# A second load of x, by positions, for the row sums of squares at the start of a hybrid decoder layer

## The chip, the cores and the metric

One core of one Trainium2 chip runs the whole layer as one program. The metric is device time in microseconds (us), median over runs. The engines are named as in the profile: PE (TensorE matmuls) and PEld (its weight loads), DVE (VectorE), ACT (ScalarE), POOL (GpSimd), SP (SyncE, whose queue issues nearly all DMAs here).

## What is computed

The reference is a layer with two token mixers and a gated MLP, float32, sequence 1024, width 1024. For the change only the first projection and the QK norm matter:

```python
def rmsnorm(x, gain):
    y = x * lax.rsqrt(jnp.mean(x * x, axis=-1, keepdims=True) + NORM_EPS)
    return y * gain

h = rmsnorm(x, mix_norm)
proj = h @ w_in                     # q, k, v, u, s, gate_a, gate_b
q = rmsnorm(q.reshape(B, S, N_Q_HEADS, HEAD_DIM), q_gain)
k = rmsnorm(k.reshape(B, S, N_KV_HEADS, HEAD_DIM), k_gain)
```

After that come banded attention (8 query heads, 2 key heads of 64), a chunked spatial gate, the output projections and a convolutional MLP.

## The kernel before, in words

All products run on PE as three float32r products, high by high, high by low, low by high (`mm3`, lines 91 to 95). So each operand is split: ACT writes the high part (`copy_hi`, line 89), DVE or POOL subtracts it for the low part. x comes transposed, in eight tiles of 128 channels by 1281 columns (a gain, 256 columns of the weights of k and v, 1024 positions).

The norm of x is applied late: the projections of the raw x times the gain are made at once, and the reciprocal root of each position (`rstd`) is multiplied in when results leave PSUM. The stage that the change touches is the first 60 us:

- **x loop** (lines 227 to 256). For each tile k: split the k/v weights (lines 229, 230) and x (233, 234), 24 matmuls into `pkv` (239), squares on ACT, a running sum on DVE (`xsquare`, 211 to 219). SP loads five tiles ahead (`X_AHEAD`). Seven matmuls on a constant stand in front (`warm`, 225).
- **q weights** `wq` in two halves (`rsplit`, 188 to 193): ACT copies, POOL subtracts. The first u weight `u0h`, `u0l` is split on ACT and DVE (258, 259).
- **Sums over channels**: eight small float32 matmuls with a column of ones (`ssq`, 321), then `rstd` (`rsqrt_cols`, 128 to 131: DVE scales, POOL takes the power -0.5).
- **k**: squares of `pkv` on ACT (334), sums on DVE (335), scaled by `rstd` squared (338), a power on POOL for each half, times `rstd` again (346); then `kr` (348), its transposition on PE (`k_trans`, 355), and the splits `k_hi`, `k_lo`, `k_twice` into `kT`.
- **q**, block by block: `q_proj` (24 matmuls into `pq`), `q_sq`, `q_ms`, `q_norm`, `q_trans`, `q_split`. `eps_x` carries the epsilon, scaled to raw x.
- **rms_rows** (135 to 143): `rstd` spread along rows by float32 matmuls into `rb`, copied to `rstd_b` by ACT.
- **v**: `v_evac` (379) and `v_split`. Then scores `sc` (`s_mm`, 439, 442), masks `c` (`s_mask`), and the u projection `pu` (`u_chunk`) as filler.

Each engine works in its own order and waits for semaphores. PE's order is the order of the source everywhere. From line 317 on (`manual_schedule`) the other engines' is too; ahead of it a scheduler orders them. PSUM has four small tiles (pool `psB`: `pq`, `pk`, `pqt`, `rb`, `warm`) and two large ones (`psA`: `pkv`, `sc`, `pu`). A DMA waits at SP until the eighth one ahead of it has landed.

Of the kernel before, what the change touches and what calls it, by code (L numbers as in the profile page):

```python
# [41 lines left out]
def body(ctx, tc, nc, a):  # L42
# [178 lines left out]
    for k in range(X_AHEAD):
        xload(k)
    warm = PH("warm")
    for _ in range(7):
        nc.tensor.matmul(warm[:, 0:128], rstd_b[:, 0:128], rstd_b[:, 0:128], start=True, stop=True)
    xcuts = {0: (slice(0, 256), slice(256, 512), slice(512, 1024))}
    for k in range(8):
        x1 = xr[k]
# [12 lines left out]
        if k > 0:  # L241
            xsquare(k - 1)
        if k + X_AHEAD < 8:
            xload(k + X_AHEAD)
        if k == 2:
            rwq = rload(a["wq"][0], "wq")
            nc.sync.dma_start(ident, a["ident"])
            nc.sync.dma_start(cp, a["cp"])
        if k == 4:
            u_raw = [wload(a["wu"][0], "wu")]  # L250
            nc.sync.dma_start(sink_b, a["sink"])
            nc.sync.dma_start(ali, a["ali"])
        if k == 5:
            rsplit(wq[0], rwq[0], 0)
    xsquare(7)
    rsplit(wq[0], rwq[1], 1)
    u_next = [wst.tile([128, 8, 128], R, tag="wh", name="u0h"), wst.tile([128, 8, 128], R, tag="wl", name="u0l")]
    copy_hi(u_next[0], u_raw[0])
    nc.vector.tensor_tensor(u_next[1], u_raw[0], u_next[0].bitcast(F), op=ALU.subtract)
# [65 lines left out]
    ss8 = pa.tile([128, 8], F, name="ss8")
    nc.vector.tensor_scalar(nsink, sink_b, -1.0, None, op0=ALU.mult)
    nc.vector.tensor_scalar(kgq, cp[:, 184:185], cp[:, 185:186], 0.125, op0=ALU.mult, op1=ALU.mult)
    nc.vector.tensor_copy(ss8, p_ssq[:, 0:16].rearrange("p (s two) -> p s two", two=2)[:, :, 0])
# [1717 lines left out]
```

## Time and profile before

| what | value |
|---|---|
| time, median of 3 runs | 1183.58 us (1183.52 to 1184.87) |
| profiled execution | span 1183.5 us (no other time of it is listed) |
| PE busy | 1170.3 us, 99% of the span |
| PEld, DVE, ACT, POOL busy | 84%, 74%, 48%, 53% |
| mean granted clock of PE | 0.998 |
| chain that ended last | PE 82%, DVE 4%, POOL 3%, ACT 2% |
| HBM read | 146.97 MB |

A group of instructions shows its start, busy time, engine, line, and out<-in; "x24" joins 24 instructions; brackets give the idle time ahead of it on its engine and what ended it. PE's busy time counts a matmul until its modelled end, so starts, not lengths, give its pace.

### The profile page before, as it was taken

What the parts mean: (1) busy time and instruction counts of PE and PEld (TensorE: products, weight loads), DVE (VectorE), ACT (ScalarE), POOL (GpSimd) and SP (SyncE); (2) the same over time, 40 slices, a digit from 0 to 9 for tenths busy, and PEclk for the clock granted to TensorE, in tenths of its full rate; (3) what the DMA queues carried; (4) which work ended last, traced back from release to release, by engine and by line L of the source; (5) the groups of instructions that cost most, each with busy time, mean ns of one, the idle gap of its engine ahead of it and who ended that gap; (6) DMA issues with size and microseconds to landing.
All of it is one profiled execution on the core that took longest, in us unless ns stands there. A gap on an engine that the chain in (4) does not pass through costs nothing.

```text
span 1183.5 us, 15928 instructions
## 1 busy us (share of the span) xinstructions
PE 1170.3 (99%) x5842; PEld 990.4 (84%) x5842; DVE 874.5 (74%) x1037; ACT 566.5 (48%) x878; POOL 631.8 (53%) x435
## 2 busy tenths in 40 slices
PE   8999999999999999999999999999999999999998
PEld 8989989988888878888878888888888888888887
DVE  7798975743536776678788788877888797875674
ACT  8555667644336653335444443444444445425331
POOL 2467685488884764444867677776767541000000
PEclk9999999999999999999999999999999999999999
DMA  7110136157556654454545445455555268975471
GB/s 272 37 55 19 54 130 228 56 168 239 161 160 204 233 193 154 146 176 132 138 129 169 118 149 152 142 141 134 166 137 160 72 219 287 365 232 196 155 231 67
DMA packets 80942, 188.66 MB, mean 159 GB/s; under 512 B 9184, under 2 KB 16864, under 8 KB 80736
## 3 DMA queue, kind: packets, MB, share of 16 engines
q1 hardware_dynamic: 73008, 167.58, 40.7%
q0 software_dynamic: 7456, 15.73, 8.0%
q10 hardware_dynamic: 400, 4.33, 1.1%
q8 instruction: 46, 0.75, 0.3%
q14 instruction: 32, 0.26, 0.1%
HBM read 146.97 MB, written 49.02 MB: 166 GB/s over the span
## 4 chain that ended last, share of the span: by engine, by line
PE 82%; DVE 4%; POOL 3%; ACT 2%; issue 2%; DMA 1%; DVEq 0%; POOLq 0%; SPq 0%; ACTq 0%
PE pz L1060 50%; PE pd L1855 10%; PE pdy L1855 8%; PE px L95 2%; PE px L93 2%; PE px L94 2%; PE pu L95 1%; PE pu L93 1%; PE pu L94 1%; PE pv L517 1%; PE pq L93 1%; PE pq L95 1%; PE pq L94 1%; DVE xa L621 1%; DMA lq<-wup 0%
## 5 line engine op out<-in xcount | busy, mean ns | idle before, releaser
L1060 PE MATMUL pz<-T,qh 128*128 128x512 f32 x472 | 145.6, 390 | 0.0
L1060 PE MATMUL pz<-B,ph 128*128 128x512 f32 x352 | 109.7, 393 | 0.7 <-ACT x L1695 0.7
L1060 PEld LDWEIGHTS pz<-T,qh 128*128 128x128 f32 x472 | 88.4, 188 | 18.6 <-ACT u L885 0.3
L1019 POOL TENSOR_TENSOR pl<-lp,ph 128x1024 fp32r<-128x1024 f32 x30 | 73.2, 2439 | 52.9 <-ACT ph L89 52.9
L1060 PE MATMUL pz<-T,ql 128*128 128x512 f32 x236 | 91.8, 389 | 0.0
L1019 POOL TENSOR_TENSOR ql<-lq,qh 128x1024 fp32r<-128x1024 f32 x30 | 76.8, 2559 | 9.1 <-ACT qh L89 9.1
L1060 PEld LDWEIGHTS pz<-B,ph 128*128 128x128 f32 x352 | 65.1, 188 | 16.7 <-ACT x L1695 3.8
L1078 DVE TENSOR_TENSOR pz<-pz,rstd_b 128x1024 f32<-128x1024 f32 x60 | 73.9, 1232 | 4.6 <-ACT rstd_b L143 2.5
L1060 PE MATMUL pz<-T,s3h 128*128 128x512 f32 x232 | 71.4, 389 | 0.0
L1060 PE MATMUL pz<-y,wjh 128*128 128x512 f32 x224 | 69.5, 391 | 0.6 <-POOL y L1233 0.3
L1060 PE MATMUL pz<-B,pl 128*128 128x512 f32 x176 | 68.6, 390 | 0.0
L1855 PE MATMUL pd<-bh,ah 128*128 128x512 f32 x176 | 68.5, 389 | 0.0
L1855 PE MATMUL pd<-bl,ah 128*128 128x512 f32 x176 | 68.5, 389 | 0.0
L1855 PE MATMUL pd<-bh,al 128*128 128x512 f32 x176 | 68.5, 389 | 0.0
L1060 PE MATMUL pz<-T,AX 128*128 128x512 f32 x264 | 63.4, 389 | 0.0
L1060 PE MATMUL pz<-B,AX 128*128 128x512 f32 x264 | 63.4, 389 | 0.0
L1019 POOL TENSOR_TENSOR s3l<-lq,s3h 128x512 fp32r<-128x512 f32 x20 | 26.0, 1298 | 62.3 <-ACT s3h L89 62.3
L1060 PEld LDWEIGHTS pz<-T,AX 128*128 128x128 f32 x264 | 49.5, 188 | 10.3
L1060 PEld LDWEIGHTS pz<-B,AX 128*128 128x128 f32 x264 | 49.6, 188 | 10.3
L89 ACT ACTIVATE AX<-lr 128x1024 fp32r<-128x1024 f32 x22 | 23.4, 1063 | 70.9 <-POOL lr L621 70.9
L621 DVE TENSOR_TENSOR pz<-pz,u 128x512 f32<-128x512 f32 x37 | 25.9, 700 | 42.5 <-ACT u L1072 36.2
L1550 DVE SCALAR_TENSOR_TENSOR tg<-pz,cp,tg 128x1023 f32<-128x1023 f32 (+1 forms) x44 | 56.2, 1278 | 0.8
(359 smaller groups left out, 3597.6 us busy)
## 6 DMA issues: line engine op xcount, KB each, us to landing
lp<-wup SPq DMA_DIRECT2D x22, 512.0 KB, 3.8
lq<-wup SPq DMA_DIRECT2D x22, 512.0 KB, 4.2
ra<-wdown SPq DMA_DIRECT2D x44, 256.0 KB, 4.9
b<-T SPq DMA_DIRECT2D x44, 256.0 KB, 3.5
lq<-wup POOLq DMA_DIRECT2D x42, 256.0 KB, 5.3
B<-tv SPq DMA_DIRECT2D x33, 256.0 KB, 2.0
T<-tt SPq DMA_DIRECT2D x33, 256.0 KB, 2.1
b<-B SPq DMA_DIRECT2D x33, 256.0 KB, 3.0
```

The costliest lines, as they stand in the source:

```text
L89: return nc.scalar.activation(dst, src, AF.Copy, scale=scale)
L93: nc.tensor.matmul(out, wh, mh, start=first, stop=False, **kw)
L94: nc.tensor.matmul(out, wh, ml, start=False, stop=False, **kw)
L95: nc.tensor.matmul(out, wl, mh, start=False, stop=last, **kw)
L517: nc.tensor.matmul(o, vhl[:, kb, g, :], w[:, 2 * g:2 * g + 2, :], start=i == 0 and g == 0, stop=i == len(ops) - 1, skip_group_check=True)
L621: eng.tensor_tensor(out, x, y, op=op)
L1019: nc.gpsimd.tensor_tensor(l, r, h.bitcast(F), op=ALU.subtract)
L1060: nc.tensor.matmul(o, p[:, k, :], m, start=not more and k == 0 and j == 0, stop=k == nk - 1 and j == 2, skip_group_check=True)
L1078: nc.vector.tensor_tensor(z, z, rstd_b, op=ALU.mult)
L1550: nc.vector.scalar_tensor_tensor(t[:, j:], p[:, 0:1024 - j], cw[:, ci, 2 - j:3 - j], t[:, j:], op0=ALU.mult, op1=ALU.add)
L1855: nc.tensor.matmul(o[d], p[:, k - k0, m], q[:, k - k0, :], start=new and k == 0 and j == 0, stop=k == HK - 1 and j == 2, skip_group_check= ...
```

## The change

x is loaded a second time, as eight tiles `xt` of 128 positions by 1024 channels, and `tsquare` squares each in one ACT pass with the sum along the row as accumulator output, into `ss8`. The running sum, the `ssq` matmuls and the copy of their result go. All eight transposed x tiles, then `wq`, `ident`, `cp`, then `xt`, `wu`, `sink_b` and `ali` stand in this order in SP's queue. The matmuls ahead of the loop are 11 in three PSUM tiles. In odd tiles DVE makes the high part of the k/v weights. The low part of `wq` moves from POOL to DVE; that of `u0` from DVE to POOL, after q's third block. k's norm takes raw sums: `krs` is `kss`/64 plus `eps_x`, to the power -0.5, so neither `rstd` squared nor the second product by `rstd` is needed; `rstd` itself is made later. The order after k's norm is written anew, and the whole stage now lies within `manual_schedule`. From the scores on, every engine has its old order.

```diff
--- before.py
+++ after.py
@@ -194,39 +193,49 @@
-    sqsum = rstd_b
+    ss8 = at.tile([128, 8], F, name="ss8")
...
-    x_first = Y("xf", F, [128, 3, 1281])
+    x_first = [Y("xf", F, [128, 3, 1281]) for _ in range(2)]
...
-    def xsquare(k):
-        for c in (L, H):
-            xs = xr[k][:, 257 + c.start:257 + c.stop]
-            if k == 0:
-                nc.scalar.activation(sqsum[:, c], xs, AF.Square)
-                continue
-            sq = PH("sq")
-            nc.scalar.activation(sq, xs, AF.Square)
-            nc.vector.tensor_tensor(sqsum[:, c], sqsum[:, c], sq, op=ALU.add)
-
-    for k in range(X_AHEAD):
+    def tload(h):
+        xt[h] = Y("xt", F)
+        for i in range(4):
+            nc.sync.dma_start(xt[h][:, i, :], a["xt"][4 * h + i])
+
+    def tsquare(t):
+        v = xt[t // 4][:, t % 4, :]
+        nc.scalar.activation(v, v, AF.Square, accum_out=ss8[:, t:t + 1])
+
+    man = tc.manual_schedule()
+    man.__enter__()
+    for k in range(8):
         xload(k)
-    warm = PH("warm")
-    for _ in range(7):
-        nc.tensor.matmul(warm[:, 0:128], rstd_b[:, 0:128], rstd_b[:, 0:128], start=True, stop=True)
+    rwq = rload(a["wq"][0], "wq")
+    nc.sync.dma_start(ident, a["ident"])
+    nc.sync.dma_start(cp, a["cp"])
+    warm = [PH("warm") for _ in range(3)]
+    for i in range(11):
+        nc.tensor.matmul(warm[i % 3][:, 0:128], rstd_b[:, 0:128], rstd_b[:, 0:128], start=True, stop=True)
...
-    for k in range(8):
+    def x_block(k):
         x1 = xr[k]
-        copy_hi(wkv[:, 0, k, :], x1[:, 1:257])
+        if k % 2:
+            nc.vector.tensor_copy(wkv[:, 0, k, :], x1[:, 1:257])
+        else:
+            copy_hi(wkv[:, 0, k, :], x1[:, 1:257])
...
+    def wq_split(c):
+        rv = rwq[c].rearrange("p (k a) b -> p k (a b)", a=2)
+        ks = slice(4 * c, 4 * c + 4)
+        nc.scalar.activation(wq[0][:, 0, ks, :], rv, AF.Copy)
+        nc.vector.tensor_tensor(wq[0][:, 1, ks, :], rv, wq[0][:, 0, ks, :].bitcast(F), op=ALU.subtract)
+
+    x_block(0)
+    x_block(1)
+    x_block(2)
+    tload(0)
+    x_block(3)
+    x_block(4)
+    x_block(5)
+    wq_split(0)
+    tload(1)
+    u_raw = [wload(a["wu"][0], "wu")]
+    nc.sync.dma_start(sink_b, a["sink"])
+    nc.sync.dma_start(ali, a["ali"])
+    x_block(6)
+    tsquare(0)
+    tsquare(1)
+    x_block(7)
+    wq_split(1)
+    for t in range(2, 8):
+        tsquare(t)
@@ -310,41 +326,30 @@
-    p_ssq = PH("ssq")
-    for s in range(8):
-        nc.tensor.matmul(p_ssq[:, 2 * s:2 * s + 2], sqsum[:, s * 128:(s + 1) * 128], ones,
-                         start=True, stop=True)
     q_proj(0)
     q_proj(1)
...
-    rsqrt_cols(rstd, ss8, 8, D)
-    nc.vector.tensor_scalar(eps_x, ss8, EPS / D, EPS * EPS, op0=ALU.mult, op1=ALU.add)
...
-    nc.vector.tensor_tensor(rstd2, rstd, rstd, op=ALU.mult)
-    nc.vector.tensor_tensor(kss3, kss3, rstd2.unsqueeze(2).to_broadcast([128, 8, 2]), op=ALU.mult)
-    rsqrt_cols(krs[:, 0:8], kss[:, 0:8], 8, 64)
-    rsqrt_cols(krs[:, 8:16], kss[:, 8:16], 8, 64)
+    nc.vector.tensor_scalar(nsink, sink_b, -1.0, None, op0=ALU.mult)
+    nc.vector.tensor_scalar(kgq, cp[:, 184:185], cp[:, 185:186], 0.125, op0=ALU.mult, op1=ALU.mult)
     q_sq(0)
+    nc.vector.tensor_scalar(eps_x, ss8, EPS / D, EPS * EPS, op0=ALU.mult, op1=ALU.add)
+    nc.vector.scalar_tensor_tensor(krs3, kss3, 1.0 / 64, eps_x.unsqueeze(2).to_broadcast([128, 8, 2]),
+                                   op0=ALU.mult, op1=ALU.add)
+    nc.gpsimd.tensor_tensor(krs[:, 0:8], krs[:, 0:8], mh05, op=ALU.pow)
+    q_ms(0)
     q_sq(1)
 
     def k_norm(h):
         ss = slice(4 * h, 4 * h + 4)
-        nc.vector.tensor_tensor(krs3[:, ss], krs3[:, ss],
-                                rstd[:, ss].unsqueeze(2).to_broadcast([128, 4, 2]), op=ALU.mult)
@@ -387,35 +392,38 @@
-    v_evac(0)
     k_norm(0)
     k_trans(0)
-    q_ms(0)
     q_ms(1)
+    nc.gpsimd.tensor_tensor(krs[:, 8:16], krs[:, 8:16], mh05, op=ALU.pow)
+    rsqrt_cols(rstd, ss8, 8, D)
+    q_norm(0)
     k_hi(0)
-    v_evac(1)
-    q_norm(0)
+    q_proj(2)
+    q_norm(1)
     k_lo(0)
-    q_norm(1)
     k_norm(1)
     k_twice(0)
-    q_proj(2)
     q_trans(0)
+    q_trans(1)
     q_split(0)
-    q_trans(1)
     q_split(1)
+    copy_hi(u_next[0], u_raw[0])
+    v_evac(0)
+    v_evac(1)
+    q_proj(3)
+    q_sq(2)
+    q_ms(2)
+    nc.gpsimd.tensor_tensor(u_next[1], u_raw[0], u_next[0].bitcast(F), op=ALU.subtract)
+    k_trans(1)
     rms_rows([PH("rb")], rstd, (0,))
-    q_proj(3)
-    k_trans(1)
+    k_hi(1)
     rms_rows([PH("rb")], rstd, (1,))
-    q_sq(2)
+    q_norm(2)
+    k_lo(1)
+    q_sq(3)
     v_split()
...
@@ -2013,6 +2021,7 @@
+        "xt": c(x.reshape(8, 128, D)),
```

**ACT between x's sixth tile and the squares of k** (`sq`: squares of x; `xt`: x by positions; `wq`: q weights; `ksq`: squares of k). Before:

```order
L218 ACTIVATE sq_435<-xr_209 128x512
L218 ACTIVATE sq_438<-xr_209 128x512
L89 ACTIVATE wkv_120<-xr_247 128x256
L89 ACTIVATE x_5_118<-xr_247 128x512
L89 ACTIVATE x_6_119<-xr_247 128x512
L218 ACTIVATE sq_441<-xr_247 128x512
L218 ACTIVATE sq_444<-xr_247 128x512
L89 ACTIVATE wq_102<-wq_251 128x1024
L89 ACTIVATE u0h<-wu_327 128x1024
L334 ACTIVATE ksq<-pkv_124 128x512
L334 ACTIVATE ksq<-pkv_125 128x512
```

and now:

```order
L254 ACTIVATE wq_102<-wq_142 128x1024
L88 ACTIVATE wkv_120<-xr_138 128x256
L88 ACTIVATE x_5_118<-xr_138 128x512
L88 ACTIVATE x_6_119<-xr_138 128x512
L219 ACTIVATE xt_254,ss_124<-xt_254 128x1024 x2
L88 ACTIVATE x_5_118<-xr_140 128x512
L88 ACTIVATE x_6_119<-xr_140 128x512
L254 ACTIVATE wq_102<-wq_144 128x1024
L219 ACTIVATE xt_254,ss_124<-xt_254 128x1024 x2
L219 ACTIVATE xt_351,ss_124<-xt_351 128x1024 x4
L338 ACTIVATE ksq<-pkv_125 128x512
L338 ACTIVATE ksq<-pkv_126 128x512
```

The squares of tiles 6 and 7 stood between splits; now two passes over `xt` stand ahead of the last x tile, six behind the second half of `wq`, and the squares of k behind these. The split of u's weight has left this place.

**DVE between the x loop and k's first normalized half** (`kss`, `krs`: k's sums and reciprocal roots; `kr`: normalized k). Before:

```order
L326 TENSOR_SCALAR nsink<-sink_b 128x8
L327 TENSOR_SCALAR kgq<-cp 128x1
L328 COPY ss_519<-ssq_460 128x8
L130 TENSOR_SCALAR rstd<-ss_519 128x8
L330 TENSOR_SCALAR eps_x<-ss_519 128x8
L335 TENSOR_REDUCE kss<-ksq 128x8 x2
L337 TENSOR_TENSOR rstd_457<-rstd 128x8
L338 TENSOR_TENSOR kss<-kss,rstd_457 128x16
L130 TENSOR_SCALAR krs<-kss 128x8 x2
L379 TENSOR_TENSOR vt<-pkv_124,rstd 128x512
L346 TENSOR_TENSOR krs<-krs,rstd 128x8
L348 TENSOR_TENSOR kr<-pkv_124,krs 128x512
```

and now:

```order
L255 TENSOR_TENSOR wq_102<-wq_144,wq_102 128x1024
L339 TENSOR_REDUCE kss<-ksq 128x8 x2
L341 TENSOR_SCALAR nsink<-sink_b 128x8
L342 TENSOR_SCALAR kgq<-cp 128x1
L344 TENSOR_SCALAR eps_x<-ss_124 128x8
L345 SCALAR_TENSOR_TENSOR krs<-kss,eps_x 128x16
L297 TENSOR_REDUCE qss_498<-qsq_493 128x4
L298 TENSOR_SCALAR qss_498<-qss_498,eps_x 128x4
L353 TENSOR_TENSOR kr<-pkv_125,krs 128x512
```

Of the steps on `rstd` none is left ahead of `kr`; `nsink`, which waits for `sink_b`, and the sums of q's first block now stand between k's sums and `kr`.

**DVE from k's second half on** (`qs`: split q; `vt`: v times `rstd`; `qss`, `qr`: sums and normalized q). Before:

```order
L289 TENSOR_TENSOR qr_564<-pq_494,qss_553 128x256
L346 TENSOR_TENSOR krs<-krs,rstd 128x8
L348 TENSOR_TENSOR kr<-pkv_125,krs 128x512
L304 TENSOR_TENSOR qs_598<-pqt_595,qs_598 64x256 x2
L304 TENSOR_TENSOR qs_606<-pqt_603,qs_606 64x256 x2
L388 TENSOR_TENSOR vhl<-vt,vhl 128x8x64 x2
L281 TENSOR_REDUCE qss_659<-qsq_653 128x4
```

and now:

```order
L353 TENSOR_TENSOR kr<-pkv_126,krs 128x512
L320 TENSOR_TENSOR qs_559<-pqt_553,qs_559 64x256 x2
L320 TENSOR_TENSOR qs_564<-pqt_556,qs_564 64x256 x2
L384 TENSOR_TENSOR vt<-pkv_125,rstd 128x512
L384 TENSOR_TENSOR vt<-pkv_126,rstd 128x512
L297 TENSOR_REDUCE qss_599<-qsq_597 128x4
L298 TENSOR_SCALAR qss_599<-qss_599,eps_x 128x4
L305 TENSOR_TENSOR qr_623<-pq_521,qss_599 128x256
```

Both `v_evac` (`vt`), of which the first stood ahead of `kr`, now follow the split of q, and the sums of q's third block stand behind them. On PE, q's fourth block ended so before (`pk`: k transposed; `rb`: `rstd` along rows; `sc`: scores):

```order
L93 MATMUL pq_617<-wq_102,x_5_118 128x256
L94 MATMUL pq_617<-wq_102,x_5_118 128x256
L95 MATMUL pq_617<-wq_102,x_5_118 128x256
L355 MATMUL pk_642<-ident,kr 128x128 x4
L140 MATMUL rb_647<-ident,rstd 128x128 x4
L439 MATMUL sc_692<-kT_107,qs_598 128x256 x2
```

and now:

```order
L94 MATMUL pq_572<-wq_102,x_5_118 128x256
L360 MATMUL pk_604<-ident,kr 128x128 x4
L139 MATMUL rb_609<-ident,rstd 128x128 x4
L139 MATMUL rb_617<-ident,rstd 128x128 x4
L447 MATMUL sc_654<-kT_107,qs_559 128x256 x2
```

The first `rb`, before ahead of q's fourth block, now stands behind `k_trans(1)`, ahead of the second, which takes the PSUM tile that `qr` of q's third block frees.

## Rows read from the trace of the kernel before

**Rows 1.** The page, busy times and the chain that ended last.

```profile
PE 1170.3 (99%) x5842; PEld 990.4 (84%) x5842; DVE 874.5 (74%) x1037; ACT 566.5 (48%) x878; POOL 631.8 (53%) x435
...
PE 82%; DVE 4%; POOL 3%; ACT 2%; issue 2%; DMA 1%; DVEq 0%; POOLq 0%; SPq 0%; ACTq 0%
```

**Rows 2.** Windows: span, five engines' busy time and count, clock, DMA share, GB/s.

```profile
5.00:10.00 5.00, 3.64 (x17) 3.03 (x18) 3.24 (x7) 4.01 (x9) 0.00 (x0) 0.82 0.96 353
...
10.00:15.00 5.00, 5.00 (x38) 5.00 (x38) 5.00 (x11) 5.00 (x11) 0.00 (x0) 0.84 1.03 399
...
6.00:7.00 1.00, 0.68 (x3) 0.48 (x4) 0.77 (x2) 0.25 (x1) 0.00 (x0) 1.00 1.05 305
...
10.00:11.00 1.00, 1.00 (x7) 1.00 (x7) 1.00 (x4) 1.00 (x3) 0.00 (x0) 0.50 1.06 436
```

**Rows 3.** Timeline of PE, 0 to 34 us: start, length, form.

```profile
1.06 3.35 PE L225 MATMUL warm<-rstd_b 128*128 128x128 f32 x14 [1.06 <-POOL mh L123]
...
6.30 0.38 PE L93 MATMUL pkv<-wkv,x 128*128 128x256 f32 x1 [1.89 <-ACT x L89]
...
11.62 0.28 PE L93 MATMUL pkv<-wkv,x 128*128 128x256 f32 x1
...
31.41 1.84 PE L321 MATMUL ssq<-ones,rstd_b 128*128 128x2 f32 x16
...
33.11 0.36 PE L93 MATMUL pq<-wq,x 128*128 128x256 f32 x1
```

**Rows 4.** Timeline of ACT, 4 to 22 and 189 us.

```profile
4.80 0.42 ACT L89 ACTIVATE wkv<-xr 128x256 fp32r<-128x256 f32 x1 [2.72 <-DMA xr<-xw]
...
15.78 1.32 ACT L89 ACTIVATE x<-xr 128x512 fp32r<-128x512 f32 x2
...
20.62 1.05 ACT L89 ACTIVATE wq<-wq 128x1024 fp32r<-128x1024 f32 x1
...
21.57 1.09 ACT L218 ACTIVATE sq<-xr 128x512 f32<-128x512 f32 x2
...
189.05 0.60 ACT L753 ACTIVATE vsh<-pvs 128x512 fp32r<-128x512 f32 x1
...
189.64 1.05 ACT L809 ACTIVATE uT<-uT 128x1024 f32<-128x1024 f32 x1
```

**Rows 5.** Timeline of DVE, POOL and ACT, 21 to 44 us.

```profile
21.75 2.44 POOL L193 TENSOR_TENSOR wq<-wq,wq 128x1024 fp32r<-128x1024 f32 x1 [18.05 <-ACT wq L89]
...
33.64 1.27 DVE L335 TENSOR_REDUCE kss<-ksq 128x8 f32<-128x512 f32 x2
...
36.11 3.25 POOL L131 TENSOR_TENSOR krs<-krs,mh 128x8 f32<-128x8 f32 x2 [0.69 <-DVE krs L130]
...
37.99 0.69 DVE L348 TENSOR_TENSOR kr<-pkv,krs 128x512 f32<-128x512 f32 x1
...
39.35 1.98 POOL L283 TENSOR_TENSOR qss<-qss,mh 128x4 f32<-128x4 f32 x2
...
42.54 0.77 ACT L89 ACTIVATE qs<-pqt 64x256 fp32r<-64x256 f32 x2 [0.38 <-PE pqt L295]
...
43.76 1.75 DVE L304 TENSOR_TENSOR qs<-pqt,qs 64x256 fp32r<-64x256 f32 x4
```

**Rows 6.** Timeline of PE, 38 to 61 us.

```profile
38.85 0.60 PE L355 MATMUL pk<-ident,kr 128*128 128x128 f32 x4
...
42.12 0.38 PE L295 MATMUL pqt<-ident,qr 128*128 128x128 f32 x2
...
44.77 0.36 PE L93 MATMUL pq<-wq,x 128*128 128x256 f32 x1 [0.37 <-DVE qs L304]
...
48.11 1.06 PE L140 MATMUL rb<-ident,rstd 128*128 128x128 f32 x8
...
48.93 0.48 PE L439 MATMUL sc<-kT,qs 128*128 128x256 f32 x2
...
60.49 0.47 PE L439 MATMUL sc<-kT,qs 128*128 128x256 f32 x2 [0.60 <-DVE c L458]
```

More of the change, by code (lines that the diff above doesn't have):

```diff
@@ L29 @@
 ROWS = (slice(0, 64), slice(64, 128))
-X_AHEAD = 5
 FILL = "qu|q|qu|qu|uu|q|qu|qu|q|qu|qu|qu|q|uu|u|u|uu|vv|v|v".split("|")
@@ L200, in body @@
     xr = {}
-    x_first = Y("xf", F, [128, 3, 1281])
+    x_first = [Y("xf", F, [128, 3, 1281]) for _ in range(2)]
     def xload(k):
-        xr[k] = x_first[:, k, :] if k < 3 else pa.tile([128, 1281], F, tag="xr", name=nm("xr"), bufs=3)
+        xr[k] = x_first[k // 3][:, k % 3, :] if k < 6 else pa.tile([128, 1281], F, tag="xr", name=nm("xr"), bufs=3)
         if k == 0:
@@ L209, in xload @@
             nc.sync.dma_start(xr[k], a["xw"][k])
-    def xsquare(k):
-        for c in (L, H):
-            xs = xr[k][:, 257 + c.start:257 + c.stop]
-            if k == 0:
-                nc.scalar.activation(sqsum[:, c], xs, AF.Square)
-                continue
-            sq = PH("sq")
-            nc.scalar.activation(sq, xs, AF.Square)
-            nc.vector.tensor_tensor(sqsum[:, c], sqsum[:, c], sq, op=ALU.add)
-    for k in range(X_AHEAD):
-        xload(k)
-    warm = PH("warm")
-    for _ in range(7):
-        nc.tensor.matmul(warm[:, 0:128], rstd_b[:, 0:128], rstd_b[:, 0:128], start=True, stop=True)
+    xt = {}
+    def tload(h):
[8 more added lines that the diff above has]
+    for k in range(8):
+        xload(k)
+    rwq = rload(a["wq"][0], "wq")
[4 more added lines that the diff above has]
+        nc.tensor.matmul(warm[i % 3][:, 0:128], rstd_b[:, 0:128], rstd_b[:, 0:128], start=True, stop=True)
     xcuts = {0: (slice(0, 256), slice(256, 512), slice(512, 1024))}
-    for k in range(8):
+    def x_block(k):
         x1 = xr[k]
-        copy_hi(wkv[:, 0, k, :], x1[:, 1:257])
+        if k % 2:
+            nc.vector.tensor_copy(wkv[:, 0, k, :], x1[:, 1:257])
+        else:
+            copy_hi(wkv[:, 0, k, :], x1[:, 1:257])
         nc.vector.tensor_tensor(wkv[:, 1, k, :], x1[:, 1:257], wkv[:, 0, k, :].bitcast(F), op=ALU.subtract)
@@ L240, in body @@
                 k == 0 and s % 2 == 0, k == 7 and s % 2 == 1)
[L241 to L259, printed above, removed]
+    def wq_split(c):
[22 more added lines that the diff above has]
+        tsquare(t)
     st = {}
@@ L312, in body @@
     krs = pa.tile([128, 16], F, name="krs")
-    rstd2 = pa.tile([128, 8], F, name="rstd2")
+    u_next = [wst.tile([128, 8, 128], R, tag="wh", name="u0h"), wst.tile([128, 8, 128], R, tag="wl", name="u0l")]
     kss3 = kss.rearrange("p (s g) -> p s g", g=2)
     krs3 = krs.rearrange("p (s g) -> p s g", g=2)
-    man = tc.manual_schedule()
-    man.__enter__()
-    p_ssq = PH("ssq")
-    for s in range(8):
-        nc.tensor.matmul(p_ssq[:, 2 * s:2 * s + 2], sqsum[:, s * 128:(s + 1) * 128], ones,
-                         start=True, stop=True)
     q_proj(0)
     q_proj(1)
[L325 to L328, printed above, removed]
-    rsqrt_cols(rstd, ss8, 8, D)
-    nc.vector.tensor_scalar(eps_x, ss8, EPS / D, EPS * EPS, op0=ALU.mult, op1=ALU.add)
     ksqs = pa.tile([128, 8, 128], F, tag="sq", name="ksq")
@@ L388, in v_split @@
             nc.vector.tensor_tensor(vl_, vg_, vh_.bitcast(F), op=ALU.subtract)
-    v_evac(0)
     k_norm(0)
     k_trans(0)
-    q_ms(0)
     q_ms(1)
+    nc.gpsimd.tensor_tensor(krs[:, 8:16], krs[:, 8:16], mh05, op=ALU.pow)
+    rsqrt_cols(rstd, ss8, 8, D)
+    q_norm(0)
     k_hi(0)
-    v_evac(1)
-    q_norm(0)
+    q_proj(2)
+    q_norm(1)
     k_lo(0)
-    q_norm(1)
     k_norm(1)
     k_twice(0)
-    q_proj(2)
     q_trans(0)
+    q_trans(1)
     q_split(0)
-    q_trans(1)
     q_split(1)
+    copy_hi(u_next[0], u_raw[0])
[6 more added lines that the diff above has]
+    k_trans(1)
     rms_rows([PH("rb")], rstd, (0,))
-    q_proj(3)
-    k_trans(1)
+    k_hi(1)
     rms_rows([PH("rb")], rstd, (1,))
-    q_sq(2)
+    q_norm(2)
+    k_lo(1)
+    q_sq(3)
     v_split()
-    q_ms(2)
-    k_hi(1)
-    k_lo(1)
     k_twice(1)
-    q_norm(2)
-    q_sq(3)
     q_ms(3)
```

## The prediction

> **What bounds the kernel now.** I read the page first: PE is busy for 99% of the span and has 82% of the chain that ended last [rows 1]. So only time that PE spends waiting, or on work that can go, is to be won. The change ends ahead of the scores, since every engine keeps its order from there on; the rest of the span can only be shifted. The windows come next: while x streams in, the queues move 353 and 399 GB/s (mean 376), and the granted clock has a mean of 0.82 and 0.84, with 0.50 inside [rows 2]. 0.18 and 0.16 of 5 us at half the clock's loss make 3.4 us at 1.2 instead of 2.4 GHz. Then PE's timeline: the constant's matmuls end at 4.41, the first `pkv` starts at 6.30, its 24 matmuls last until 11.62, and the other 168 until 31.41 at 0.118 us each; so the clock was low from 8.2 to 11.6. `ssq` takes the 1.70 to 33.11 [rows 3]. Two q blocks follow, without a gap worth naming, to `k_trans(0)` at 38.85. Behind it come waits of 0.60 us or less: at the second transposition of q (it is behind what PE started at 42.12), at 44.77, and at the third score tile, 60.49 [rows 6]. In the timelines of ACT, DVE and POOL the reader is to see what a step of the norm costs: POOL's power on 8 columns 1.63, on 4 columns 0.99, `kr` 0.69 [rows 5].
>
> **What goes.** `ssq` costs PE 1.7. The power of `rstd`, which ended 0.69 ahead of k's at 36.11 [rows 5], and the products by it leave the way to `kr`; of k's two powers only the first, 1.63 of the 3.25, was on it. The 14 half-tile squares on ACT (1.09 for two, [rows 4]) and their additions on DVE go too; they lay beside PE's matmuls and by themselves save nothing. The low halves of `wq` leave POOL (2.44 each, [rows 5]) for DVE, hidden beside the x loop, where DVE has the time of the removed additions.
>
> **What comes: the second load.** This is the term that decides. SP's queue holds eight x tiles of 656 kB, two halves of `wq` of 524, 165 of `ident` and `cp`, then eight `xt` of 524: 10,655 kB to the last `xt`. The first 656 kB had landed by 4.80 [rows 4]. At 376 GB/s the other 9,999 take 26.6, so the last `xt` lands at 31.4. `wu` and `sink_b` behind it land near 32.8; `nsink`, which waits for `sink_b` on DVE, now stands ahead of `krs`, with some 1.4 us to spare. The bounds of the pace are 305 (the slowest microsecond) and 436 GB/s (the fastest) [rows 2], which put the last `xt` at 37.6 and 27.7. The mean over ten microseconds of the same stream is the nearest row, so I take it.
>
> Here a page speaks against the change. The Trainium skill's "DMA: Bandwidth & Descriptors", section "Where 436 GB/s comes from", says that for transfers between HBM and SBUF the HBM side binds, at about 358 GB/s per core. An estimate by it puts the last `xt` at 32.7 and my time at 1184.5; the row's 399 over five microseconds doesn't bear that limit out, so the sum keeps 376.
>
> **ACT's chain.** A pass `tsquare` of 1024 lies between 0.95 (the `wq` copy, 20.62 to 21.57) and 1.24. The square with a row sum at L753 takes 0.59 for 512, 189.05 to 189.64 [rows 4], against 0.50 to 0.55 without one; so I take 0.95 plus 0.09, 1.04. ACT's order puts the second `xt` ahead of the last x tile: it lands at 4.80 + 6,855/376 = 23.0, its pass ends at 24.1, the x tile's two copies take 1.22 (1.32 for the pair, less the 0.10 by which ACT's rows overlap the next), `wq` 0.95 and six passes 6.24, so ACT is done at 32.5. By the last landing it is 31.4 + 1.04 = 32.4: queue and engine end together. Then two squares of k, 0.5 each, to 33.5; the second sum on DVE, 0.64, to 34.2; four small steps. Before, three or four such steps filled the 0.69 in which POOL waited ahead of 36.11 [rows 5]; I take 0.7, to 34.9. POOL's power 1.63, `kr` 0.69 and 0.17 of handing on (38.68 to 38.85 before, [rows 5, 6]) put `k_trans(0)` at **37.5**, 1.35 earlier.
>
> **PE ahead of it.** Eleven constant matmuls at 0.48 (3.35 over 7, [rows 3]) hold PE until 6.3, when x waits already; 240 matmuls at 0.118 with no low clock end at 34.6. PE waits about 2.9 us for k, where it now waits for nothing: the removed `ssq` and the 2.5 us lost in the first block don't reach the end. That is most of what the change could give.
>
> **Behind it.** `q_proj(2)` follows, and the first transposition of q starts 3.27 after `k_trans(0)` as before (38.85 to 42.12, [rows 6]), at 40.8; the powers of its q now end on POOL near 38.6, two of 0.99 behind k's, so q is ready ahead of PE. The waits of 0.60 and 0.37 go. But both `rb` now stand behind `k_trans(1)`, and the second takes a PSUM tile that `qr` of q's third block must free. DVE reaches that after splitting q (ACT 0.77, four steps of DVE 1.75, [rows 5]) and both `v_evac`, 0.69 each, which no longer stand ahead of `kr`: splits done at 43.3, v at 44.7, the sums at 45.3, POOL's power at 46.3, `qr` and the handing on by 47.2. PE finishes q's fourth block, `k_trans(1)` and the first `rb` by 45.3, so it waits 1.9 us. The scores start at 48.0 instead of 48.93: 0.9 of the 1.35 is left and the new wait eats the rest and the two stalls. `u0l` on POOL, 2.44, stands behind that power and ends near 49; its reader `pu` stands behind the first scores and 24 matmuls of 2.8, so nothing waits. At 60.49 the wait of 0.60 for DVE's mask goes if DVE, with v done ahead, is early; ends 0 and 0.7, and I take 0.7, since `q_ms`, `k_lo` and `v_evac` have left the place ahead of it. **Sum without the clock: 0.9 + 0.7 = 1.6 us gained**, which the PE-paced rest carries to the end.
>
> **The clock.** The one PE wait of over a microsecond in these rows, 4.41 to 6.30, with sparse work behind it, was followed by the low clock 3.8 us after PE had stopped. The waits of 0.60 and 0.37 were followed by none. A wait of 2.9 us is longer than the one that was followed by 1.2 GHz, so I expect a low stretch here too. It lasted 3.4 us and half of PE's work in it is lost: at most 1.7. If it began as PE stopped, only 0.5 us of it would lie behind `k_trans(0)`: 0.25. Since the fall in the row came after the wait had ended, I take a value nearer the upper end, **1.2**. Everything behind hangs on `q_proj(2)` and moves with it. The rule that bears on it, from the Trainium skill's "TensorE: Matmul & The Clock Gate", section "What's actually happening", is that the default state is throttled and activity releases it; the row above agrees, and no page changes the sum here.
>
> **Forecast:** 1.6 less 1.2 is a gain of 0.4. The profiled span is 1183.5, 0.1 below the median 1183.58; against the median the forecast is **1183.2**. Chance 0.38.
>
> **Rivals.**
> - *The clock holds* through the wait, or PE is later and waits less (a low stretch at the start as before would bring PE to k at 37): 1183.6 - 1.6 = **1182.0**. For it: no row shows a fall after a wait with dense work on both sides. Against: the wait is half as long again as the one before the fall. Chance 0.25.
> - *The second load is slow.* Every microsecond by which the last `xt` lands later than 31.4 moves `k_trans(0)` and all behind it. At 305 GB/s that is 6.2 us: **1189.4**. It decides against the change from a landing 0.4 later, 371 GB/s, and is more than 2.4 us slower than before from 34.2 on, 340 GB/s. For it: the stream is two thirds longer than before and runs beside ACT's and DVE's own traffic; against it, the 399 in a stretch where all engines were busy. Chance of over 2.4 slower 0.12; of a milder case, 371 to 340 GB/s, 0.10, whose middle at 356 lands the last `xt` at 32.9 and gives 1184.7. The page on DMA named above states such a pace; the time here is worked out from landings.
> - *The stream is fast and ACT's chain is all.* At 436 GB/s the second `xt` lands at 20.5, ACT ends at 30.0 and `kr` comes 2.5 earlier; PE's wait shrinks to 0.4 and no clock falls: 1182.0 - 2.5 = **1179.5**. For it, the single microsecond at 436; against it, no five microseconds had it. Chance 0.15.
>
> **How the numbers follow.** A measurement of this kernel can tell some 0.2%, 2.4 us, from no change. Forecast, the held clock but for its tail, and the milder case of a slow load lie within it; below 1181.2 lie the fast stream and the tail of the held clock (an `rb` wait that isn't there gives up to 0.9 more): 0.15 + 0.08 = 0.23. Slower than 1186.0 is the slow stream, 0.12. The range goes from 1180.0, which takes in most of the fast cases, to 1185.8, a stream at 342 GB/s or two low stretches of 1.7, and leaves out about 2 in 10.
>
> **What would show it.** In the changed profile `k_trans(0)` should start near 37.5 behind a PE wait of 2 to 4 us that ends with DVE's `kr`, no `ssq`, ACT's last `tsquare` near 32.5 right after the last `xt` lands, a low clock between 36 and 42 and none at 8 to 12, a PE wait of about 2 ahead of the second `rb`, and no wait at the third score tile. A full clock there means the first rival; passes on ACT that wait for `xt`, with landings past 33, the second; ACT busy without a break before the end, with `xt` landed by 28, the third. I am wrong altogether if PE doesn't wait for k, or if the order from the scores on loses what was won.

## The result, and the profile after

The changed kernel takes 1185.93 us (median of 16 runs, 1184.79 to 1188.17), the kernel before 1184.20 in the same comparison (16 runs, 1183.52 to 1185.66). The ratio is 1.0016, 95% interval 1.0009 to 1.0023: slower by 1.7 us. The forecast was 1183.2 with a range up to 1185.8.

In every run that lists both, the time is 1.7 above the span (1185.73 with a span of 1184.0 in the profiled run of the change). So the profile shown of before, with its span of 1183.5, is of an execution of about 1185.2 (an estimate), one microsecond above the median of its kernel. A profile is of one execution only: below, those of e1, e2 and e4 have the lowest time of their runs, those of e3 and e7 the highest.

The page of the changed kernel, busy times and the chain that ended last:

```profile
PE 1169.9 (99%) x5834; PEld 991.2 (84%) x5834; DVE 865.2 (73%) x1022; ACT 566.2 (48%) x874; POOL 629.5 (53%) x434
...
PE 89%; DVE 2%; POOL 2%; DMA 2%; issue 1%; ACT 1%; SPq 0%; DVEq 0%; POOLq 0%; ACTq 0%
```

Little shows there: PE is as busy as in [rows 1], with a larger share of the chain (89 instead of 82%). The windows of the first 50 us tell more (columns as in [rows 2]):

```profile
0.00:5.00 5.00, 3.94 (x19) 3.94 (x20) 0.89 (x2) 2.42 (x4) 2.96 (x10) 1.00 0.58 188
5.00:10.00 5.00, 4.71 (x38) 4.26 (x37) 3.66 (x8) 2.94 (x6) 0.00 (x0) 1.00 1.00 357
10.00:15.00 5.00, 5.00 (x44) 5.00 (x44) 4.91 (x10) 4.76 (x9) 0.00 (x0) 1.00 1.03 422
15.00:20.00 5.00, 5.00 (x45) 5.00 (x44) 2.28 (x5) 0.41 (x2) 0.00 (x0) 1.00 1.02 394
...
35.00:40.00 5.00, 1.73 (x12) 1.53 (x11) 3.28 (x13) 0.95 (x3) 3.40 (x3) 0.90 0.05 20
40.00:45.00 5.00, 5.00 (x36) 5.00 (x36) 2.90 (x5) 3.15 (x7) 3.48 (x3) 0.76 0.00 0
```

The low clock has left the start (0.82 and 0.84 in [rows 2], 1.00 now) and come back at 35 to 45 us (0.90 and 0.76): again 3.4 us at 1.2 GHz. PE is busy for 1.73 of the 5 us from 35 on. ACT does next to nothing from 15 to 20. PE's timeline:

```profile
5.35 0.37 PE L92 MATMUL pkv<-wkv,x 128*128 128x256 f32 x1
...
38.65 0.81 PE L360 MATMUL pk<-ident,kr 128*128 128x128 f32 x4 [3.27 <-DVE kr L353]
...
43.48 0.60 PE L311 MATMUL pqt<-ident,qr 128*128 128x128 f32 x4
...
47.09 1.06 PE L139 MATMUL rb<-ident,rstd 128*128 128x128 f32 x8
...
49.98 1.16 PE L139 MATMUL rb<-ident,rstd 128*128 128x128 f32 x8 [1.83 <-DVE qr L305]
...
50.89 0.48 PE L447 MATMUL sc<-kT,qs 128*128 128x256 f32 x2
...
61.84 0.47 PE L447 MATMUL sc<-kT,qs 128*128 128x256 f32 x2
```

PE starts 0.95 earlier than in [rows 3] and has no `ssq`, then waits 3.27 us for `kr`. `k_trans(0)` starts at 38.65, 0.2 earlier than in [rows 6]; the first transposition of q 1.36 later (43.48 against 42.12), the scores 1.96 later (50.89 against 48.93), the third score tile 1.35 later (61.84 against 60.49). What ACT, POOL and DVE did:

```profile
19.93 1.06 ACT L254 ACTIVATE wq<-wq 128x1024 fp32r<-128x1024 f32 x1 [4.59 <-DMA wq<-wq]
...
22.99 1.06 ACT L219 ACTIVATE xt<-xt 128x1024 f32<-128x1024 f32 x1 [0.46 <-DMA xt<-xt]
...
24.27 1.06 ACT L219 ACTIVATE xt<-xt 128x1024 f32<-128x1024 f32 x1
...
32.70 1.04 ACT L219 ACTIVATE xt<-xt 128x1024 f32<-128x1024 f32 x1
...
33.74 1.06 ACT L338 ACTIVATE ksq<-pkv 128x512 f32<-128x512 f32 x2
...
36.20 1.68 POOL L347 TENSOR_TENSOR krs<-krs,mh 128x8 f32<-128x8 f32 x1 [32.49 <-DVE krs L345]
...
46.50 1.29 DVE L384 TENSOR_TENSOR vt<-pkv,rstd 128x512 f32<-128x512 f32 x2
...
49.50 0.42 DVE L305 TENSOR_TENSOR qr<-pq,qss 128x256 f32<-128x256 f32 x1 [1.12 <-POOL qss L299]
```

ACT waits 4.59 us for the first half of `wq`, with x's seventh tile, which had landed at 15.57 by the trace, behind that in its order; its last square ends at 33.74, POOL's power starts at 36.20. The norm of q's third block comes behind both `vt`, and the second `rb` waits for it.

### The profile page after: what moved, and what is told of

Same layout as the page of the kernel before. It is cut to its first block, busy times and chain, and to the rows that moved or that the text cites. A ratio compares the mean times of both kernels' runs of the same rounds, so it can differ in the third digit from the quotient of the medians.

```text
span 1184.0 us, 15888 instructions
## 1 busy us (share of the span) xinstructions
PE 1169.9 (99%) x5834; PEld 991.2 (84%) x5834; DVE 865.2 (73%) x1022; ACT 566.2 (48%) x874; POOL 629.5 (53%) x434
## 4 chain that ended last, share of the span: by engine, by line
PE 89%; DVE 2%; POOL 2%; DMA 2%; issue 1%; ACT 1%; SPq 0%; DVEq 0%; POOLq 0%; ACTq 0%
PE pz L1068 53%; PE pd L1863 10%; PE pdy L1863 8%; PE px L94 2%; PE px L92 2%; PE px L93 2%; PE pvs L93 1%; PE pvs L94 1%; PE pvs L92 1%; PE pu L94 1%; PE pu L92 1%; PE pu L93 1%; DMA xf<-xw 1%; DMA xt<-xt 1%; PE pq L92 1%
## 5 line engine op out<-in xcount | busy, mean ns | idle before, releaser
L1558 DVE SCALAR_TENSOR_TENSOR tv<-pz,cp,tv 128x1023 f32<-128x1023 f32 (+1 forms) x44 | 56.3, 1279 | 0.8
```

Of the source, the lines that this page charges most:

```text
L1558: nc.vector.scalar_tensor_tensor(t[:, j:], p[:, 0:1024 - j], cw[:, ci, 2 - j:3 - j], t[:, j:], op0=ALU.mult, op1=ALU.add)
```

## The experiments

Times are against the kernel before in the same comparison; the changed kernel is +1.73 on this scale.

| run | against before, us | ratio and interval |
|---|---|---|
| e1 q's third block twice | +1.9 | 1.0018 (1.0009 to 1.0027) |
| e2 q's third block first | +1.6 | 1.0017 (1.0008 to 1.0025) |
| e3 its norm ahead of v | -0.9 | 0.9994 (0.9986 to 1.0003) |
| e4 no second load | +4.3 | 1.0042 (1.0028 to 1.0056) |
| e5 e2, two PSUM tiles at the start | -0.3 | 0.9996 (0.9987 to 1.0005) |
| e6 e5 and e3 | -1.1 | 0.9992 (0.9984 to 1.0001) |
| e7 e4 and e3, two tiles | -0.5 | 0.9997 (0.9988 to 1.0006) |
| e8 the change, one tile | +2.8 | 1.0026 (1.0015 to 1.0036) |
| e9 e1, two tiles | -0.4 | 0.9996 (0.9988 to 1.0005) |
| e10 another order on ACT | -2.4 | 0.9981 (0.9972 to 0.9990) |
| e11 e10 and e3 | -4.2 | 0.9966 (0.9953 to 0.9978) |
| e12 before, once more | -0.5 | 0.9996 (0.9987 to 1.0005) |

**The first four.** e1 keeps PE busy in the wait, e2 moves work into it, e3 takes the wait at the second `rb` away, e4 undoes the second load.

e1 and e2 (e2 also drops the later `q_proj(2)`):

```diff
+    q_proj(2)
     k_norm(0)
     k_trans(0)
```

> PE computes q's third block once more, into the same PSUM tile, while it waits for k at 35.2 to 38.7 us (24 matmuls, 2.8 us); everything else is as in the changed kernel. Theory (the wait lets the granted clock fall, and that costs half of 3.4 us): no low clock behind 39 us, the first transposition of q 1.7 earlier (near 41.8), and a time 1.7 below the changed kernel, so level with the kernel before. Rival (the clock falls for another reason, or what it costs is given back in the wait ahead of the second rb): 1.7 above the kernel before, as the changed kernel is.

> q's third block is projected ahead of the transposition of k instead of behind it. Theory (PE's wait for k and the low clock it brings are the cost): the wait shrinks from 3.3 to about 0.5 us, the clock stays at 2.4 GHz and PE stands 2.8 + 1.7 us further on behind it, but the wait ahead of the second rb, which hangs on ACT, DVE and POOL, grows to about 3 us; so some 1.7 to 2.2 below the changed kernel, level with the kernel before. Rival (PE's place decides alone): 4.5 below the changed kernel.

e3:

```diff
     q_trans(1)
+    q_sq(2)
+    q_ms(2)
     q_split(0)
     q_split(1)
+    q_norm(2)
     copy_hi(u_next[0], u_raw[0])
     v_evac(0)
     v_evac(1)
     q_proj(3)
-    q_sq(2)
-    q_ms(2)
...
     rms_rows([PH("rb")], rstd, (1,))
-    q_norm(2)
```

> The sums of q's third block and its norm stand on ACT, DVE and POOL ahead of v's evacuation and of the copy of u's weight. Theory (the second rb waits 2 us for a PSUM tile that this norm frees, behind v): that wait of 1.8 goes, the scores start near 48.9 instead of 50.9, and the time is about 1.8 below the changed kernel, level with the kernel before. Rival (the wait is only moved to the scores or to the mask): less than 0.7 below the changed kernel.

e4, at the end of the x loop and behind it:

```diff
     x_block(7)
+    xsquare(6)
+    xsquare(7)
     wq_split(1)
-    for t in range(2, 8):
-        tsquare(t)
...
+    for s in range(8):
+        nc.tensor.matmul(p_ssq[:, 2 * s:2 * s + 2], sqsum[:, s * 128:(s + 1) * 128], ones,
+                         start=True, stop=True)
     q_proj(0)
```

> The second load of x is undone: squares of the transposed tiles with the running sum and the 16 small matmuls as before, all else (order of the queue, scaled epsilon, order behind k's norm) as changed. Theory (k's norm waits for the second load and ACT's passes behind it): PE reaches the transposition of k at 36.8 without a wait, the clock stays at 2.4 GHz, the second rb still waits about 2 us, the scores start near 47.3 and the time is 3.6 below the changed kernel, 1.9 below the kernel before. Rival (the order behind k's norm is the cost, not the load): within 0.7 of the changed kernel.

e3 came out as its theory said, and by more: 2.6 below the changed kernel instead of 1.8. In its profile the wait at the second `rb` is gone, but the scores start at 49.87, not near 48.9: this execution took 1185.92, and its low clock lasts longer (told at the end). The other three missed. In e1's profile all that it was meant to do is there: the windows from 35 to 45 us have a clock of 1.00 (the second is below), k's transposition waits 0.68 us, and the third score tile starts at 59.03, 2.8 earlier than in the changed kernel. Its time was still the changed kernel's. A window of e1, then PE's timeline, which shows where it went:

```profile
40.00:45.00 5.00, 5.00 (x46) 4.93 (x45) 4.67 (x10) 3.66 (x8) 2.18 (x2) 1.00 0.02 5
```

```profile
37.35 0.66 PE L362 MATMUL pk<-ident,kr 128*128 128x128 f32 x4 [0.68 <-DVE kr L355]
...
59.03 0.48 PE L451 MATMUL sc<-kT,qs 128*128 128x256 f32 x2
...
220.65 0.74 PE L1072 MATMUL pz<-x,ph 128*128 128x512 f32 x2 [1.62 <-DVE vg L772]
```

The first gate product `pz` waits 1.62 us for DVE's `vg`, far behind the change; DVE's timeline of e1 has that `vg` right ahead of it:

```profile
219.85 0.75 DVE L772 SCALAR_TENSOR_TENSOR vg<-pvs,vss,sg_b 128x512 f32<-128x512 f32 x1
```

PE's timeline of e4 has the same, and one more:

```profile
217.56 0.39 PE L92 MATMUL pm<-wgh,vsh 128*128 128x256 f32 x1 [0.53 <-ACT pm L941]
...
220.83 0.73 PE L1075 MATMUL pz<-x,ph 128*128 128x512 f32 x2 [1.62 <-DVE vg L775]
```

The changed kernel itself has no wait there; its `pz` starts, right behind the product ahead of it, at:

```profile
221.42 0.63 PE L1068 MATMUL pz<-x,ph 128*128 128x512 f32 x2
```

The four small PSUM tiles are given out in turn, from the constant's matmuls at the start on. Each tile more or less, and each exchange in the order, shifts which of them every later product gets; when the pool of small tiles is closed, `pz` takes over two of them. By the programs' PSUM addresses these two held the fifth and sixth v tile in the changed kernel. In e1, e2 and e4 they include the last v tile, which DVE empties last (the expectations of e5 and e8 say the last but one).

**Is it the PSUM tile?** e5 and e8 change only the number of tiles of the constant's matmuls, against e2 and against the changed kernel (2 in e5, as below, and 1 in e8):

```diff
-    warm = [PH("warm") for _ in range(3)]
+    warm = [PH("warm") for _ in range(2)]
     for i in range(11):
-        nc.tensor.matmul(warm[i % 3][:, 0:128], rstd_b[:, 0:128], rstd_b[:, 0:128], start=True, stop=True)
+        nc.tensor.matmul(warm[i % 2][:, 0:128], rstd_b[:, 0:128], rstd_b[:, 0:128], start=True, stop=True)
```

> As the run with q's third block ahead of the transposition of k (e2), but with two PSUM tiles instead of three for the 11 constant matmuls at the start. That alone shifts which of the four small PSUM tiles each later product gets. Theory (e1, e2 and e4 lost what they gained at 218 to 221 us, since there the first gate product pz takes the PSUM tile that the second-last v tile frees late, 1.78 us of PE waiting): here pz takes a tile that is freed two tiles earlier, the wait goes, and the time is 1.8 below e2, 1184.0, level with the kernel before. Rival (the wait only shows a lateness that comes from elsewhere): unchanged from e2, 1.6 above the kernel before.

> The changed kernel with one PSUM tile instead of three for the 11 constant matmuls, nothing else. By its program pz now waits for the tile of the last but one v product, as in e2. Theory (which PSUM tile pz takes is worth up to 1.8 us, whatever happens in the first 60 us): 1 to 1.8 above the changed kernel, 2.7 to 3.5 above the kernel before. Rival (the tile doesn't matter, since PE comes later there): as the changed kernel, 1.7 above the kernel before.

e5 is 1.9 below e2, e8 1.1 above the changed kernel, both as the theory said. PE's timeline of e5, then of e8:

```profile
219.57 0.63 PE L1068 MATMUL pz<-x,ph 128*128 128x512 f32 x2
```

```profile
222.25 0.73 PE L1068 MATMUL pz<-x,ph 128*128 128x512 f32 x2 [1.61 <-DVE vg L768]
```

So experiments on the start have to be read with this tile in view. In e5, e6, e7 and e9 to e11 `pz` does not wait.

In e2, e5 and e6 the clock fell all the same, against what e2 and e6 were expected to show. With q's third block gone from behind it, PE meets four waits close together, here in PE's timeline of e2:

```profile
37.04 0.65 PE L360 MATMUL pk<-ident,kr 128*128 128x128 f32 x4 [0.84 <-DVE kr L353]
...
38.03 0.44 PE L311 MATMUL pqt<-ident,qr 128*128 128x128 f32 x2 [0.34 <-DVE qr L305]
...
39.18 0.44 PE L311 MATMUL pqt<-ident,qr 128*128 128x128 f32 x2 [0.71 <-DVE qr L305]
...
40.81 0.36 PE L92 MATMUL pq<-wq,x 128*128 128x256 f32 x1 [1.20 <-DVE kT L374]
```

and the windows of e2 show the clock behind them:

```profile
40.00:45.00 5.00, 4.18 (x23) 4.22 (x24) 4.83 (x10) 3.36 (x7) 1.87 (x2) 0.66 0.01 2
```

The wait was split up and moved, not filled. The wait ahead of the second `rb`, which e2's expectation had growing to 3 us, is gone in its profile: both `rb` run through from 45.68.

**The clock.** e9 is e1 with two tiles, so that `pz` doesn't wait.

> e1 (q's third block computed twice, so that PE is busy while it waits for k) with two PSUM tiles instead of three at the start, so that pz takes a tile that is freed early. Against the changed kernel it then differs by the clock alone. Theory (the wait for k costs a low clock of 3.4 us, and half of the work in it): no low clock at 38 to 45 us and 1.7 below the changed kernel, 1184.2, level with the kernel before. Rival (the clock's price is taken back by later waits): as the changed kernel, 1.7 above.

It came to 1184.18, as expected, 2.1 below the changed kernel (by the two intervals, give or take 1.3). The windows of e9:

```profile
35.00:40.00 5.00, 5.00 (x45) 5.00 (x45) 2.96 (x11) 1.49 (x3) 4.14 (x4) 1.00 0.03 13
40.00:45.00 5.00, 5.00 (x45) 4.85 (x44) 4.46 (x8) 4.47 (x9) 2.74 (x2) 1.00 0.01 2
```

The matmuls that fill the wait do nothing that is kept; they hold the clock at 1.00, where the changed kernel has 0.90 and 0.76, and that is worth about 2 us. This is not one profile's doing: in all 22 runs of e1 and e9 the mean granted clock is 0.999 or 1.000, in the sixteen of the changed kernel 0.995 to 0.999 but for one. e9 also has two tiles where the change has three; `pz` waits in neither, but the change with two tiles was not run.

**Without the load, with the rest mended.**

> e5 and e3 together: q's third block ahead of the transposition of k, its sums and norm ahead of v's evacuation, two PSUM tiles at the start. Theory: no wait at the second rb and none at pz, the clock stays high up to the scores, the scores start near 47, and the time is 0.7 below the kernel before. Rival (ACT and DVE bound the stretch from 37 to 48 us, whatever their order): as e5.

> e4 (no second load, running sums as before) with the sums of q's third block ahead of v's evacuation and with two PSUM tiles at the start, after which pz waits for no tile. Theory: the waits of 1.9 at the second rb and of 1.8 at pz go, so the time is 3.3 below e4, 1185.2, or, by e4's profile against that of the kernel before, about 2 below the kernel before. Rival (e4 is slow for another reason, the squares on ACT and their sums on DVE): less than 1.5 below e4.

e6 is 1.1 below the kernel before (0.7 expected), with an interval that still touches 1, and that with a low clock that it was not to have. e7 is 4.8 below e4, more than the 3.3 expected (the two waits are 1.45 and 1.62 in e4's profile); why e4 was that slow is not settled by its profile. But e7 can be set beside e3, which keeps the load, has q's third norm in the same place and no wait at `pz` either: 0.5 and 0.9 below the kernel before. So taking the load out wins nothing that these runs resolve, and the load by itself is not what makes the change slow.

**ACT's order.** e10 leaves the load as changed and gives ACT another order, and DVE what follows from it: x's last two tiles go ahead of `wq` and of all row squares, the squares of k ahead of the last two.

```diff
     x_block(5)
-    wq_split(0)
...
     x_block(6)
-    tsquare(0)
-    tsquare(1)
     x_block(7)
+    wq_split(0)
     wq_split(1)
-    for t in range(2, 8):
+    for t in range(6):
         tsquare(t)
...
         nc.scalar.activation(ksq, pk4[h][:, :, 0:128], AF.Square)
...
+    tsquare(6)
+    tsquare(7)
     nc.vector.tensor_scalar(nsink, sink_b, -1.0, None, op0=ALU.mult)
```

> The changed kernel with another order on ACT only: x's last two tiles ahead of the q weights and of all row squares (ACT sat idle from 15.4 to 19.9 us for the q weights while x's seventh tile had landed), and the squares of k ahead of the last two row squares, so that their sums on DVE lie beside ACT. Theory (k's norm is late by ACT's order, 2.7 us of the 3.3 that PE waits): the last row square ends near 33 with k's sums done, k is transposed at 36, PE waits under 1 us, the clock stays high, and the time is 4.3 below the changed kernel, 2.5 below the kernel before. Rival (the landing of the last tiles bounds it): 0.7 below the changed kernel, and the clock still falls.

> e10 and e3 together: the other order on ACT, and the sums and the norm of q's third block ahead of v's evacuation. Theory: no long wait of PE is left in the first 60 us, the scores start near 45 to 46, and the time is 5 to 6 below the changed kernel, 3.3 to 4 below the kernel before. Rival (what is won in the first 60 us is given back by the waits at 215 to 222 us): as e10 or less than 1 below the kernel before.

e10 is 2.4 below the kernel before (2.5 expected), e11 4.2 below it (3.3 to 4 expected): at 1180.42 it beats both kernels, interval 0.9953 to 0.9978 (five runs). ACT and POOL of e10, then PE and a window:

```profile
16.83 2.60 ACT L88 ACTIVATE x<-xr 128x512 fp32r<-128x512 f32 x4
...
20.17 1.06 ACT L254 ACTIVATE wq<-wq 128x1024 fp32r<-128x1024 f32 x1 [0.74 <-DMA wq<-wq]
...
30.73 1.07 ACT L336 ACTIVATE ksq<-pkv 128x512 f32<-128x512 f32 x2
...
32.72 1.05 ACT L219 ACTIVATE xt<-xt 128x1024 f32<-128x1024 f32 x1
...
34.36 1.67 POOL L347 TENSOR_TENSOR krs<-krs,mh 128x8 f32<-128x8 f32 x1 [30.66 <-DVE krs L345]
```

```profile
36.81 0.66 PE L360 MATMUL pk<-ident,kr 128*128 128x128 f32 x4 [1.06 <-DVE kr L353]
```

```profile
40.00:45.00 5.00, 4.99 (x42) 4.66 (x41) 4.67 (x10) 3.16 (x7) 1.64 (x2) 1.00 0.01 2
```

The last square still starts at 32.72 (32.70 in the changed kernel), but k's squares and sums no longer stand behind it: POOL's power starts at 34.36 instead of 36.20, `k_trans(0)` at 36.81 instead of 38.65, and no low clock follows. So e10 takes back both the late k and what the clock cost. PE's timeline of e11:

```profile
36.56 0.66 PE L360 MATMUL pk<-ident,kr 128*128 128x128 f32 x4 [1.52 <-DVE kr L353]
...
43.60 1.95 PE L139 MATMUL rb<-ident,rstd 128*128 128x128 f32 x16
45.31 0.48 PE L447 MATMUL sc<-kT,qs 128*128 128x256 f32 x2
```

A wait of 1.52 us is left; no low clock follows it, both `rb` run through, and the scores start at 45.31, 5.6 earlier than in the changed kernel.

**Before, once more.**

> The kernel before, once more, as a measure of what the comparison resolves and of how far two of its profiled executions differ. Within 0.1% of itself. If the matmuls of the gate input at 180 to 212 us run at a spacing of 0.118 instead of the 0.113 of the first profile, that spacing belongs to the execution and not to the program; if they run at 0.113 again, the program may set it.

It differs from itself by 0.04%, and the comparison resolves about 0.1%. The spacing is told of at the end.

## Why the prediction was wrong

Forecast: a gain of 0.4; measured: a loss of 1.7. The waits and the low clock came as described; the landing rule behind the first and the price of the second were off, and so was the base.

- **"K's norm, ACT's chain": the step that failed.** The sum put `k_trans(0)` at 37.5 (its terms add up to 37.4); it came at 38.65. The passes cost what was said: six in 6.24 from 27.50 on, 1.04 each. What was late is the second `xt`, 23.0 forecast, 24.27 in the trace, and all behind it on ACT. I had reckoned a landing as all bytes ahead over the pace. The windows from 5 to 20 us show a pace of 391 GB/s in the mean (357, 422 and 394), above the 376 taken, and by 20 us they had moved 6.8 MB; up to the first half of `wq` the queue held 5.8. Yet that half landed at 19.91, not at the 18.4 that this rule gives. The trace records a landing in sixteen parts: fifteen of this half's were there by 18.66, the last came 1.25 later, and pieces of later tiles had gone past by then. In e1 and e2, where the last part is 0.3 behind, the same copy starts at 18.59 and 18.29 and `k_trans(0)` at 37.35 and 37.04, so the rule holds in some executions and not in others; what holds the last part up stays open. This comes nearest to the rival of a slow second load in its mild form (1184.7), by another mechanism: the pace was not lower, and the last `xt` landed at 31.93, only 0.5 behind the forecast.
- **"Queue and engine end together" was read too kindly.** It was nearly true of the last square, which started at 32.70, 0.8 behind its landing, and not of the norm: e10 starts the last square at the same time and POOL's power 1.8 earlier. That ACT would idle there (4.59 us) could be read from the order of the program, before any trace of the change.
- **"The clock": right in kind, too small.** The low stretch lasted 3.4 us, as forecast, and came behind the wait for k: the clock was still 1.00 when PE started again at 38.65, and fell at 39.0, as these windows of the changed kernel show:

```profile
38.50:39.00 0.50, 0.35 (x3) 0.35 (x4) 0.46 (x3) 0.00 (x0) 0.36 (x1) 1.00 0.00 0
39.00:39.50 0.50, 0.50 (x5) 0.50 (x4) 0.50 (x3) 0.01 (x1) 0.23 (x1) 0.52 0.00 0
```

  From `k_trans(0)` to the first transposition of q it took 4.83 instead of 3.27 us: 1.56 of price, where I took 1.2 between 0.25 and 1.7. e9 makes it 2.1 in the time. That the wait brings the low clock, and not something else in the change, is shown by e1 and e9, which fill it. The Trainium skill's "TensorE: Matmul & The Clock Gate", section "What's actually happening", has throttled as the default state and activity as what releases it; the trace agrees in so far as the low clock follows PE's idle 3.27 us.
- **"Behind it": right.** The second `rb` waits 1.83 (1.9 forecast); from the first transposition of q to it 6.5 us (6.4 forecast); e3, which moves the sums ahead of u's copy on ACT and of v on DVE, removes the wait. The third score tile waits no more for the mask (the lag falls from 1.96 at the scores to 1.35 there: 0.6 won, 0.7 forecast). `pu` waits for no `u0l`.
- **The sum.** Scores forecast at 48.0 + 1.2 = 49.2, measured 50.89. Of the 1.7 between, 1.15 is the late k and 0.36 the clock. Behind them little changes: the scores are 1.96 later than before, `pz` is 1.67 later (221.42 against the line of before below), and the time is 1.73 longer.

```profile
219.75 0.63 PE L1060 MATMUL pz<-x,ph 128*128 128x512 f32 x2
```

- **The base.** My 1183.58 was the median of three runs; that of sixteen is 1184.20, which alone took 0.6 off the forecast. And the profiled span, which I set 0.1 below the median, is 1.7 below its own run's time.
- **DMA pace.** From 10 to 15 us the queues moved 422 GB/s, so the pace was no cause. The Trainium skill's "DMA: Bandwidth & Descriptors", section "Where 436 GB/s comes from", has HBM bind at about 358 GB/s per core; this trace does not bear that out, and the estimate by it, 1184.5, was nearer to the time than mine for another reason.

## What to carry to other kernels

When work is moved off an engine that bounds the kernel, write down the order on each of the engines that get it, and look for the step that is waited for behind a wait for something else: here the whole loss of 1.7 us, and 2.4 more, lay in where x's last two tiles, a weight copy and four of the eight squares stood on ACT (e10). The wait of 3.3 us cost PE its length and then half of a further 3.4 us, and matmuls that nobody needs bought the second part back. Before an experiment is believed, its profile is read to the end: here a gain at 60 us was lost at 220, by a change in the number or the order of PSUM tiles far ahead.
